# w_down in two column blocks at a time, with seven products for eight in half of its pairs of k-tiles

## The chip, the core and the metric

The kernel runs on one core of a Trainium2 chip. The metric is the time of one execution on the device, in microseconds (us). Five engines work side by side: TensorE (PE, matrix products), VectorE (DVE), ScalarE (ACT), GpSimd (POOL) and SyncE (SP). Each takes its own instructions in the order in which the program issues them, and waits on semaphores for the others. SP issues nearly all loads of weights, POOL issues the transfers that add to what they find.

## The reference

One block of a streaming encoder, for x of 256 rows (S) by 2048 columns (D), in float32. First `h = x + W_out [attention ; convolution](rms_norm(x))`, and then the part that changes, the gated feed-forward network with 5632 hidden columns:

```python
hn   = rms_norm(h, norm2_g)
gate = hn @ w_gate            # 256 x 5632, k = 2048
up   = hn @ w_up              # 256 x 5632, k = 2048
a    = silu(gate) * up
out  = h + a @ w_down         # 256 x 2048, k = 5632
```

## The kernel before

**Three matmuls for a product.** Every float32 operand is split into a high part in the matmul's own type (a cast on ACT) and a low part (DVE subtracts the cast from the original). A product of a k-tile (128 rows of k) is three matmuls of 128 x 128 by 128 x 512: high by high, low by high, high by low.

**Columns and groups.** w_gate and w_up are taken in 11 blocks `j` of 512 columns, w_down in four blocks `n` of 512. The hidden columns are used in groups of 4, 4 and 3 blocks (`FGROUPS`): gate and up of j = 0 to 3, then w_down over their 16 k-tiles for all four `n`; then j = 4 to 7 and w_down; then j = 8 to 10 and w_down over 12 k-tiles. The result gathers in DRAM: it holds h first, and the first two groups add their share by an accumulating DMA on POOL's queue (`down_done`, L1034, after a copy on ACT, L1033). The last group instead fetches what is there (`fetch_sums`, L1025, on SP's queue, ahead of the loads that follow it), adds on DVE (L1043) and writes.

**Seven products for eight.** In the blocks j = 1 to 10 four pairs of k-tiles are computed by a scheme that needs seven block products for the eight of a 2 x 2 block product (rows: the two halves of 128 rows; columns: gate and up). Such an "s" unit loads four weight tiles at once (`load_pair`, L898, tile `wb`, 1 MB). DVE forms four sums of them (`round_pair`, L907 to L909, tile `wt`), ACT casts the three tiles of `wb` that are used directly and the four sums (L910, L911, tile `wh`), DVE takes the seven low parts (`split_pair`, L915 for those of `wb`, L916 for the sums, tile `wl`), and PE runs 21 matmuls (L932 to L934) into seven PSUM banks. The left side of these products is prepared once, by `make_forms` (tiles `fhi`, `flo`). The rest of a block are plain units of two k-tiles and 12 matmuls, "g" for gate and "u" for up. A capital letter in `ORDER = "sgGsgGsUUsUu"` marks a unit whose low part is made by DMA: ACT writes the negated original, and POOL's queue adds the original to the cast from DRAM. A block is 180 matmuls. At its end DVE combines the banks (`products_done`, L995 to L1004, and `block_done`, L1013, L1015).

**Transposes.** The block's result `a` must stand with k on the partitions for w_down. `transposed` does that two k-tiles at a time during the next block: PE transposes four tiles into one bank (`ps_a`, L827), ACT casts the high part (`ahi`, L829), DVE takes the low part (`alo`, L831).

**w_down** uses plain units alone: 12 matmuls for two k-tiles (L356, L357, L362), one block of columns after another, all low parts on DVE (L326).

**The order of the work.** All units stand in one list, and `run_chunks` goes through it. At step t it issues the load of unit t + 5, for a capital unit also the cast and the accumulating DMA of unit t + 5, the cast of unit t + 3, the low parts of unit t + 2, and the matmuls of unit t. The ends of blocks and the transposes are generators, which move one step each time PE's code calls `resume()`, several times in a unit. So the order on each engine is set when the program is written, and an operation that waits holds up all that stands behind it on its engine.

**Buffers.** Two `wb`, one `wt`, two `wh`, two `wl`, five `raw` (loads of plain units), four each of `whi` and `wlo`. All eight PSUM banks are in use: four `acc`, four `aux`, of which the transposes take one while a block is under way.

Of the kernel before, what the change touches and what calls it, by code (L numbers as in the profile page):

```python
# [18 lines left out]
P = 128  # L19
# [38 lines left out]
RAW_BUFS = 5  # L58
# [24 lines left out]
PRODUCTS = ((Q1, 0, 5), (Q6, 5, 1), (Q7, 6, 2), (Q5, 4, 3), (Q2, 1, 6), (Q4, 3, 0), (Q3, 2, 4))  # L83

LOAD_AHEAD, DMA_AHEAD, HI_AHEAD, LO_AHEAD = 5, 5, 3, 2
# [15 lines left out]
def tile_block(  # L101
# [11 lines left out]
    lhs = ctx.enter_context(tc.tile_pool(name="lhs", bufs=KD // 2))  # L113
# [95 lines left out]

    halves = {}  # L210
# [6 lines left out]
    def lhs_two(pfx, k):  # L217
        return tuple(lhs.tile([P, 2, S], F32R, tag=f"l{x}", name=f"{pfx}{x}{k}") for x in ("hi", "lo"))
# [165 lines left out]
    def run_chunks():  # L384
        n = len(chunks)
        loaded = split = 0
# [14 lines left out]
        for t in range(n):  # L401
# [17 lines left out]
            if t in fetch_at:  # L419
                fetch_sums(fetch_at[t])  # L420
# [336 lines left out]
    def out_done(n, ps):  # L757
# [28 lines left out]
        if n == D // N - 1:  # L786
            yield
            for m in range(NM):
                ss = small.tile([P, 1], F32, tag="ssh", name="ssh")
                dve.tensor_reduce(ss, ss2[m], AX.X, ALU.add)  # L790
                rsqrt_mean(rstd2[m], ss, D, EPS)
            yield
            yield
            prestack.close()
            ffn["pool"] = ctx.enter_context(tc.tile_pool(name="ffn", bufs=1))
            start(make_forms())
# [22 lines left out]

    def transposed(j, aa):  # L820
        for t in range(N // P // 2):
# [6 lines left out]
            hi, lo = lhs_two("a", j * (N // P) + 2 * t)  # L828
            act.copy(hi, pt)  # L829
            yield from lag(2)  # L830
            dve.tensor_tensor(lo, pt, hi.bitcast(F32), ALU.subtract)  # L831
            for i in range(2):
                actT[j * (N // P) + 2 * t + i] = (hi[:, i, :], lo[:, i, :])
            yield from lag(2 if j else 1)

    forms = {}

    def make_forms():  # L840
# [33 lines left out]
        f = fp.tile([P, 7, NS, P], F32, tag="wh", name="sums", bufs=2)  # L874
        dve.scalar_tensor_tensor(f[:, 4], a21, -1.0, a22, ALU.mult, ALU.subtract)
        dve.scalar_tensor_tensor(f[:, 5], f[:, 4], -1.0, a11, ALU.mult, ALU.subtract)
        act.copy(fhi[:, 0], a11)
        act.copy(fhi[:, 1], a12)
        act.activation(fhi[:, 3], a22, AF.Copy, scale=-1.0)
        yield  # L880
        dve.tensor_tensor(f[:, 6], a11, a21, ALU.subtract)
        dve.tensor_tensor(f[:, 2], a12, f[:, 5], ALU.subtract)
        act.copy(fhi[:, 4:7], f[:, 4:7])
        act.copy(fhi[:, 2], f[:, 2])
# [4 lines left out]
        dve.scalar_tensor_tensor(flo[:, 3], a22, -1.0, fhi[:, 3].bitcast(F32), ALU.mult, ALU.subtract)  # L889
        dve.tensor_tensor(flo[:, 2], f[:, 2], fhi[:, 2].bitcast(F32), ALU.subtract)  # L890
        yield
        dve.tensor_tensor(flo[:, 4:7], f[:, 4:7], fhi[:, 4:7].bitcast(F32), ALU.subtract)
        forms.update(hi=fhi, lo=flo)

    def load_pair(c):
        c["b"] = early.tile([P, 4, N], F32, tag="wb", name="wb")
        src = weights([(w, k, c["col"], N) for w in ("w_up", "w_gate") for k in (c["k"], c["k"] + HK)])
# [14 lines left out]

    def split_pair(c):
        c["lo"] = ffn["pool"].tile([P, 7, N], F32R, tag="wl", name="wl", bufs=2)
        dve.tensor_tensor(c["lo"][:, 4:], c["b"][:, 1:], c["hi"][:, 4:].bitcast(F32), ALU.subtract)  # L915
        dve.tensor_tensor(c["lo"][:, :4], c["t"], c["hi"][:, :4].bitcast(F32), ALU.subtract)  # L916
# [8 lines left out]
    def multiply_pair(c):  # L925
        while "hi" not in forms:
            resume()
        fhi, flo, p = forms["hi"], forms["lo"], c["k"]
        for n, (q, f, w) in enumerate(c["products"]):
# [4 lines left out]
            pe.matmul(ps, fhi[:, f, p, :], c["lo"][:, w], start=False, stop=bool(last))  # L934
# [6 lines left out]
    def multiply_two(c):  # L941
        hi, lo = c["hi"], c["lo"]
        qs = (Q3, QX) if c["kind"] == "u" else (Q2, Q4)
        for i, k in enumerate(c["ks"]):
            x1, x2 = forms["plain"][k]
            for m, q in enumerate(qs):
                ms = slice(m * P, (m + 1) * P)
                ps = sum_bank(c, q)
                pe.matmul(ps, x1[:, ms], hi[:, i, :], start=i == 0 and bool(c["first"].get(q)), stop=False)  # L949
                pe.matmul(ps, x2[:, ms], hi[:, i, :], start=False, stop=False)  # L950
        resume()
        for m, q in enumerate(qs):
            ms = slice(m * P, (m + 1) * P)
            for i, k in enumerate(c["ks"]):
                pe.matmul(sum_bank(c, q), forms["plain"][k][0][:, ms], lo[:, i, :], start=False,  # L955
                          stop=i == 1 and bool(c["last"].get(q)))
# [4 lines left out]
    def fast_block(j, order, after_down):  # L961

        units, sums = [], {}
        left = dict(s=list(range(NS)), g=list(TWOS), u=list(TWOS))
        for unit in order:
            kind = unit.lower()
            what = left[kind].pop(0)
            c = dict(kind=kind, sums=sums, done=None, first={}, last={})
            if kind == "s":
                c.update(k=what, col=j * N, by_dma=False, load=load_pair, round=round_pair, split=split_pair,  # L970
                         multiply=multiply_pair, uses=[q for q, _, _ in PRODUCTS], products=PRODUCTS)
            else:
                c.update(ks=what, w="w_gate" if kind == "g" else "w_up", nk=2, width=N, cols=[(j * N, N)],
                         by_dma=unit.isupper(),
                         load=load_chunk, round=round_chunk, split=split_chunk, multiply=multiply_two,
                         uses=(Q3, QX) if kind == "u" else (Q2, Q4))
            units.append(c)
        assert not any(left.values())
        if after_down:

            units[0]["products"] = PRODUCTS[4:] + PRODUCTS[:4]
        for q in range(8):
            users = [c for c in units if q in c["uses"]]
            users[0]["first"][q] = users[-1]["last"][q] = True
        [c for c in units if c["kind"] == "s"][-1]["done"] = products_done
        units[-1].update(done=lambda sums: block_done(j, sums), prompt=True)
        chunks.extend(units)
# [3 lines left out]
    def products_done(q):  # L991
# [11 lines left out]
        act.activation(w1, w1, AF.Silu)  # L1003
        dve.tensor_tensor(u3, q[Q4], u3, ALU.add)  # L1004
        act.activation(u3, u3, AF.Silu)
        halfway.update(g=(w1, u3), u=(u2, w4))

# [11 lines left out]
    so_far, fetch_at = {}, {}  # L1019

    def fetch_sums(n):
        so_far[n] = []
        for m in range(NM):
            t = ffn["pool"].tile([P, N], F32, tag=f"sum{n % 2 * NM + m}", name="so_far")
            sp.dma_start(out=t, in_=out[m * P : (m + 1) * P, n * N : (n + 1) * N])  # L1025
            so_far[n].append(t)

    def down_done(g, n, ps):
        cs = slice(n * N, (n + 1) * N)
        if g < len(FGROUPS) - 1:  # L1030
            for m in range(NM):
                t = ffn["pool"].tile([P, N], F32, tag=f"sum{n % 2 * NM + m}", name="part")
                act.copy(t, ps[m])  # L1033
                pool.dma_start(out=out[m * P : (m + 1) * P, cs], in_=t, accum_op=ALU.add)  # L1034
            return
        parts = 2 if n == D // N - 1 else 1
        for m in range(NM):
            t = so_far[n][m]
# [89 lines left out]
```

## Time and profile before

| | |
|---|---|
| time, median of 3 runs | 1079.25 us (1078.09 to 1081.81) |
| profiled execution | 1078.51 us, of which the profile's span is 1076.7 us |
| PE busy | 1051.7 us, 98% of the span |
| DVE busy | 801.4 us, 74% |
| ACT busy | 618.0 us, 57% |
| POOL busy | 110.4 us, 10% |
| TensorE clock granted | 0.995 of full speed |
| data moved by DMA | 236.57 MB, 220 GB/s in the mean |

Times are in microseconds from the span's start unless marked otherwise. L912 is line 912 of the kernel before, or, in rows of the changed kernel, of that one; the two are numbered apart. In a row such as `out<-in`, the names are the program's tiles; `q` are the PSUM banks of a gate/up block, `acc` those of a w_down unit. A busy PE need not be a PE at its peak, since matmuls overlap; the step from one start to the next is what a matmul costs.

### The profile page before, as it was taken

To read this page: it belongs to the slowest core of one execution; us is meant where nothing else is said; L and a number is where in the kernel's file an instruction comes from. 1 tells how busy PE (TensorE), PEld (TensorE's weight loads), DVE (VectorE), ACT (ScalarE), POOL (GpSimd) and SP (SyncE) were. 2 spreads that over 40 slices of the span, in tenths; PEclk is the share of its full clock that TensorE was granted. 3 is DMA by queue.
4 is the path that set the end of the run, shared out by engine and by line. 5 is a ranking of instruction groups with operands and counts; after the bars stand their busy time and mean duration, and the time that the engine had idled before them with its cause. 6 is when DMAs were issued, how large, how long until landed. Compare 5 with 4: busy or idle time off the path is not lost. (4 is left out here: it accounts for less than half of the span.)

```text
span 1076.7 us, 13151 instructions
## 1 busy us (share of the span) xinstructions
PE 1051.7 (98%) x4834; PEld 870.9 (81%) x4834; DVE 801.4 (74%) x979; ACT 618.0 (57%) x811; POOL 110.4 (10%) x155
## 2 busy tenths in 40 slices
PE   8999999999999999999999999999999999999798
PEld 7988888877888887788888878878888878888686
DVE  4799988899666689988644688889745477897353
ACT  6544566756756557757343667586544474765231
POOL 0130112200100100101000111010001010100000
PEclk9999999999999999999999999999999999999899
DMA  9555555344457568898476898988847799887471
GB/s 314 205 176 180 200 189 176 137 176 151 143 190 242 175 228 252 284 304 244 153 232 197 267 295 252 293 221 268 259 157 201 239 277 319 223 273 208 145 278 66
DMA packets 62781, 236.57 MB, mean 220 GB/s; under 512 B 7044, under 2 KB 8510, under 8 KB 57596
## 3 DMA queue, kind: packets, MB, share of 16 engines
q1 hardware_dynamic: 52320, 202.66, 52.1%
q0 software_dynamic: 10336, 33.04, 16.6%
q8 instruction: 38, 0.62, 0.2%
q14 instruction: 27, 0.22, 0.1%
q10 hardware_dynamic: 60, 0.03, 0.0%
HBM read 227.30 MB, written 8.39 MB: 219 GB/s over the span
## 5 line engine op out<-in xcount | busy, mean ns | idle before, releaser
L317 ACT CAST whi<-raw 128x1024 fp32r<-128x1024 f32 (+1 forms) x297 | 305.8, 1050 | 183.2 <-PE acc L357 98.1
L326 DVE TENSOR_TENSOR wlo<-raw,whi 128x1024 fp32r<-128x1024 f32 (+1 forms) x249 | 299.7, 1219 | 142.8 <-ACT whi L317 140.9
L357 PE MATMUL acc<-whi,alo 128*128 128x512 f32 x384 | 150.5, 392 | 6.6 <-DVE alo L831 6.6
L356 PE MATMUL acc<-whi,ahi 128*128 128x512 f32 x384 | 150.4, 392 | 0.0
L356 PE MATMUL acc<-whi,xhi 128*128 128x512 f32 (+1 forms) x352 | 131.0, 378 | 3.2 <-ACT xhi L223 2.4
L357 PE MATMUL acc<-whi,xlo 128*128 128x512 f32 (+1 forms) x352 | 129.5, 374 | 0.5 <-DVE xlo L224 0.4
L949 PE MATMUL q<-whi,chi 128*128 128x512 f32 x320 | 124.7, 390 | 0.0
L950 PE MATMUL q<-whi,clo 128*128 128x512 f32 x320 | 124.6, 389 | 0.0
L932 PE MATMUL q<-wh,fhi 128*128 128x512 f32 x280 | 109.7, 392 | 1.7 <-DVE alo L831 1.7
L934 PE MATMUL q<-wl,fhi 128*128 128x512 f32 x280 | 109.0, 389 | 0.0
L933 PE MATMUL q<-wh,flo 128*128 128x512 f32 x280 | 109.0, 389 | 0.0
L512 DVE SCALAR_TENSOR_TENSOR y<-upad,cw,y 128x256 f32<-128x256 f32 x240 | 103.7, 483 | 4.4 <-ACT y L505 3.9
L362 PE MATMUL acc<-wlo,ahi 128*128 128x512 f32 x384 | 103.6, 391 | 0.0
L911 ACT CAST wh<-wt 128x2048 fp32r<-128x2048 f32 x40 | 76.5, 1912 | 38.3 <-DVE wt L909 37.6
L916 DVE TENSOR_TENSOR wl<-wt,wh 128x2048 fp32r<-128x2048 f32 x40 | 91.7, 2291 | 6.6 <-ACT wh L911 5.9
L915 DVE TENSOR_TENSOR wl<-wb,wh 128x1536 fp32r<-128x1536 f32 x40 | 70.1, 1754 | 27.9 <-ACT wh L910 27.9
L357 PEld LDWEIGHTS acc<-whi,alo 128*128 128x128 f32 x384 | 72.6, 189 | 22.1 <-DVE alo L831 6.9
L362 PE MATMUL acc<-wlo,xhi 128*128 128x512 f32 (+1 forms) x352 | 88.3, 376 | 1.4 <-DVE wlo L326 1.4
L955 PE MATMUL q<-wlo,chi 128*128 128x512 f32 x320 | 86.6, 392 | 2.8 <-DMA wlo<-in_wts_dram 2.8
L356 PEld LDWEIGHTS acc<-whi,ahi 128*128 128x128 f32 x384 | 72.5, 189 | 15.3 <-ACT ahi L829 0.2
L362 PEld LDWEIGHTS acc<-wlo,ahi 128*128 128x128 f32 x384 | 71.7, 188 | 14.6
L356 PEld LDWEIGHTS acc<-whi,xhi 128*128 128x128 f32 x352 | 67.2, 191 | 14.9 <-ACT xhi L223 2.8
(197 smaller groups left out, 1487.2 us busy)
## 6 DMA issues: line engine op xcount, KB each, us to landing
raw<-in_wts_dram SPq DMA_DIRECT2D x295, 512.0 KB, 4.9
wb<-in_wts_dram SPq DMA_DIRECT2D x40, 1024.0 KB, 6.2
wlo<-in_wts_dram POOLq DMA_DIRECT2D x48, 512.0 KB, 8.3
out_dram<-part POOLq DMA_DIRECT2D x16, 256.0 KB, 5.1
out_dram<-h POOLq DMA_DIRECT2D x8, 256.0 KB, 5.9
so_far<-out_dram SPq DMA_DIRECT2D x8, 256.0 KB, 4.4
h<-in_x_dram SPq DMA_DIRECT2D x6, 256.0 KB, 7.6
out_dram<-so_far POOLq DMA_DIRECT2D x6, 256.0 KB, 3.0
```

Source lines behind the costliest of these rows:

```text
L317: act.copy(c["hi"], c["raw"])
L326: dve.tensor_tensor(c["lo"], c["raw"], c["hi"].bitcast(F32), ALU.subtract)
L356: pe.matmul(ps[m], xhi[:, ms], hi[:, j, :], start=c["first"] and j == 0, stop=False)
L357: pe.matmul(ps[m], xlo[:, ms], hi[:, j, :], start=False, stop=False)
L362: pe.matmul(ps[m], xhi[:, ms], lo[:, j, :], start=False, stop=c["last"] and j == nk - 1)
L512: dve.scalar_tensor_tensor(y[:, ct, :], src, wk, y[:, ct, :], ALU.mult, ALU.add)
L916: dve.tensor_tensor(c["lo"][:, :4], c["t"], c["hi"][:, :4].bitcast(F32), ALU.subtract)
L932: pe.matmul(ps, fhi[:, f, p, :], c["hi"][:, w], start=bool(first), stop=False)
L933: pe.matmul(ps, flo[:, f, p, :], c["hi"][:, w], start=False, stop=False)
L934: pe.matmul(ps, fhi[:, f, p, :], c["lo"][:, w], start=False, stop=bool(last))
L949: pe.matmul(ps, x1[:, ms], hi[:, i, :], start=i == 0 and bool(c["first"].get(q)), stop=False)
L950: pe.matmul(ps, x2[:, ms], hi[:, i, :], start=False, stop=False)
```

## The change

1. w_down takes two blocks of columns at a time (`down_block`). The two take the place of up and gate in a block: four pairs of k-tiles in each of the first two groups and three in the last become s units with seven products for eight, the other half stays plain. The matmuls of w_down go from 1056 to 990, and there are 62 s units in all instead of 40. Some of the plain units have their low parts by DMA now (capitals in `DOWN`): 72 in the whole program instead of 48.
2. The transposed result that goes into an s unit of w_down needs forms like those of `make_forms`. `pair_forms` makes them: ACT copies the bank out (`af`), casts three of its quarters, DVE forms four sums (`fs`), ACT casts these, DVE takes the low parts.
3. The low parts of an s unit are split in two tiles that are made at two times. `split_pair` makes four of them (`wla`, two buffers: one of `wb`, three of the sums), `split_rest` the other three (`wlb`, one buffer: one of the sums, two of `wb`). `split_rest` is called one unit ahead of the unit's matmuls, or by the next `round_pair` if that comes first.
4. All groups add their sums to DRAM by POOL's accumulating DMA, but for the last block of columns of the last group: its sum so far is fetched by one DMA of 512 KB on POOL's queue (`down_products`), added on DVE and written by SP. Copies on ACT before the accumulating DMAs are gone.
5. The order of the products after a w_down group is no longer turned round; two of the seven left forms change places; there are four `raw` buffers instead of five; the left side's tiles stand in one fixed array.

```diff
-RAW_BUFS = 5
+RAW_BUFS = 4
-PRODUCTS = ((Q1, 0, 5), (Q6, 5, 1), (Q7, 6, 2), (Q5, 4, 3), (Q2, 1, 6), (Q4, 3, 0), (Q3, 2, 4))
+PRODUCTS = ((Q1, 0, 5), (Q6, 5, 1), (Q7, 6, 2), (Q5, 4, 3), (Q2, 1, 6), (Q4, 2, 0), (Q3, 3, 4))
+DOWN = (dict(pairs=((0, 0), (0, 1), (1, 0), (1, 1)), order="sgGsgGsUusUu"),
+        dict(pairs=((4, 0), (4, 1), (5, 0), (5, 1)), order="sgGsgGsUusUu"),
+        dict(pairs=((8, 0), (8, 1), (9, 0)), order="sgGsGsUuU"))
...
@@ run_chunks
-            if t in fetch_at:
-                fetch_sums(fetch_at[t])
+            while rest < min(n, t + 1 + REST_AHEAD):
+                split_rest(chunks[rest])
+                rest += 1
             chunks[t]["multiply"](chunks[t])
...
@@ transposed
+            if (j, t) in d["pairs"]:
+                yield from pair_forms(j, t, pt)
+            else:
+                hi, lo = d["at"][j, t]
+                act.copy(hi, pt)
+                yield from lag(2)
+                dve.tensor_tensor(lo, pt, hi.bitcast(F32), ALU.subtract)
...
+    def pair_forms(j, t, pt):
...
+        a = fp.tile([P, 2, NM, P], F32, tag="sum0", name="af")
+        act.copy(a, pt)
+        a11, a21, a12, a22 = a[:, 0, 0], a[:, 0, 1], a[:, 1, 0], a[:, 1, 1]
+        act.copy(fhi[:, :2], a[:, :, 0])
+        act.activation(fhi[:, 2], a22, AF.Copy, scale=-1.0)
+        yield
+        f = fp.tile([P, 4, P], F32, tag="sum2" if j else "sum1", name="fs")
+        dve.scalar_tensor_tensor(f[:, 1], a21, -1.0, a22, ALU.mult, ALU.subtract)
+        dve.scalar_tensor_tensor(f[:, 2], f[:, 1], -1.0, a11, ALU.mult, ALU.subtract)
+        dve.tensor_tensor(f[:, 3], a11, a21, ALU.subtract)
+        dve.tensor_tensor(f[:, 0], a12, f[:, 2], ALU.subtract)
+        act.copy(fhi[:, 3:], f)
+        yield
+        dve.tensor_tensor(flo[:, :2], a[:, :, 0], fhi[:, :2].bitcast(F32), ALU.subtract)
+        dve.scalar_tensor_tensor(flo[:, 2], a22, -1.0, fhi[:, 2].bitcast(F32), ALU.mult, ALU.subtract)
+        yield
+        dve.tensor_tensor(flo[:, 3:], f, fhi[:, 3:].bitcast(F32), ALU.subtract)
...
     def round_pair(c):
+        if newest:
+            split_rest(newest.pop())
+        newest.append(c)
...
     def split_pair(c):
-        c["lo"] = ffn["pool"].tile([P, 7, N], F32R, tag="wl", name="wl", bufs=2)
-        dve.tensor_tensor(c["lo"][:, 4:], c["b"][:, 1:], c["hi"][:, 4:].bitcast(F32), ALU.subtract)
-        dve.tensor_tensor(c["lo"][:, :4], c["t"], c["hi"][:, :4].bitcast(F32), ALU.subtract)
+        if "lo" in c:
+            return
+        b, t, hi = c["b"], c["t"], c["hi"].bitcast(F32)
+        lo = ffn["pool"].tile([P, 4, N], F32R, tag="wla", name="wla", bufs=2)
+        dve.tensor_tensor(lo[:, 0], b[:, 2], hi[:, 5], ALU.subtract)
+        dve.tensor_tensor(lo[:, 1:], t[:, 1:], hi[:, 1:4], ALU.subtract)
...
+    def split_rest(c):
+        if "sides" not in c or 0 in c.get("lo", ()):
+            return
+        split_pair(c)
+        b, t, hi = c["b"], c["t"], c["hi"].bitcast(F32)
+        lo = ffn["pool"].tile([P, 3, N], F32R, tag="wlb", name="wlb")
+        dve.tensor_tensor(lo[:, 1], t[:, 0], hi[:, 0], ALU.subtract)
+        dve.tensor_tensor(lo[:, ::2], b[:, 1::2], hi[:, 4::2], ALU.subtract)
...
+    def down_block(g, n):
...
+        units = fast_block(DOWN[g]["order"], ("w_down", n * N), ("w_down", (n + 1) * N),
+                           [(q, ks(jt)) for q, jt in enumerate(pairs)], [(jt, ks(jt)) for jt in twos],
...
-    def fetch_sums(n):
-        so_far[n] = []
-        for m in range(NM):
-            t = ffn["pool"].tile([P, N], F32, tag=f"sum{n % 2 * NM + m}", name="so_far")
-            sp.dma_start(out=t, in_=out[m * P : (m + 1) * P, n * N : (n + 1) * N])
...
+    def down_products(n, q, last):
+        so_far = None
+        if last:
+            so_far = ffn["pool"].tile([P, 4, N], F32, tag="wt", name="so_far")[:, :NM]
+            pool.dma_start(out=so_far, in_=out[:, n * N : (n + 1) * N].rearrange("(m p) n -> p m n", p=P))
+        yield from bank_sums(q)
+        for m in range(NM):
+            add_to_out(m, n + 1, halfway["g"][m])
...
     for g, nb in enumerate(FGROUPS):
...
-        for n in range(D // N):
-            block("w_down", n * N, range(j0 * 4, (j0 + nb) * 4), fa, lambda ps, g=g, n=n: down_done(g, n, ps))
+        for n in range(0, D // N, 2):
+            down_block(g, n)
```

Three places show how the rows move. The first is DVE in the gate/up block j = 4, from its first s unit on. Before:

```order
L907 TENSOR_TENSOR wt<-wb 128x1024
L908 TENSOR_TENSOR wt<-wb,wt 128x512
L909 TENSOR_TENSOR wt<-wt,wb 128x512
L915 TENSOR_TENSOR wl<-wb,wh 128x1536
L916 TENSOR_TENSOR wl<-wt,wh 128x2048
L326 TENSOR_TENSOR wlo<-raw,whi 128x1024
```

And in the changed program:

```order
L964 TENSOR_TENSOR wt<-wb 128x1024
L965 TENSOR_TENSOR wt<-wb,wt 128x512
L966 TENSOR_TENSOR wt<-wt,wb 128x512
L978 TENSOR_TENSOR wla<-wb,wh 128x512
L979 TENSOR_TENSOR wla<-wt,wh 128x1536
L337 TENSOR_TENSOR wlo<-raw,whi 128x1024
L988 TENSOR_TENSOR wlb<-wt,wh 128x512
L989 TENSOR_TENSOR wlb<-wb,wh 128x2x512
```

Between the last sum and the first low part that needs the cast sums there stood 1536 columns of other work (L915), now there stand 512 (L978); two of the three pieces on `wb` come last (L989).

The second place is DVE at the start of the last w_down group, from the end of the last gate/up block on. Before (`alo` are the low parts of that block's transposes):

```order
L1015 TENSOR_TENSOR sum_8332<-sum_8332,sum_8331 128x512
L1015 TENSOR_TENSOR sum_8334<-sum_8334,sum_8333 128x512
L326 TENSOR_TENSOR wlo<-raw,whi 128x1024 x4
L831 TENSOR_TENSOR alo_8420<-ps_a,ahi_8419 128x512
L326 TENSOR_TENSOR wlo<-raw,whi 128x1024 x2
L831 TENSOR_TENSOR alo_8469<-ps_a,ahi_8468 128x512
```

And in the changed program, where `llo` is what `alo` was:

```order
L1127 TENSOR_TENSOR sum_8559<-sum_8559,sum_8558 128x512
L1127 TENSOR_TENSOR sum_8561<-sum_8561,sum_8560 128x512
L964 TENSOR_TENSOR wt<-wb 128x1024
L965 TENSOR_TENSOR wt<-wb,wt 128x512
L966 TENSOR_TENSOR wt<-wt,wb 128x512
L978 TENSOR_TENSOR wla<-wb,wh 128x512
L979 TENSOR_TENSOR wla<-wt,wh 128x1536
L988 TENSOR_TENSOR wlb<-wt,wh 128x512
L989 TENSOR_TENSOR wlb<-wb,wh 128x2x512
L964 TENSOR_TENSOR wt<-wb 128x1024
L965 TENSOR_TENSOR wt<-wb,wt 128x512
L966 TENSOR_TENSOR wt<-wt,wb 128x512
L867 TENSOR_TENSOR llo<-ps_a,lhi 128x512
```

The first transposed tiles' low part (L867) stands behind one s unit's sums and low parts and the sums of the next.

The third place is ACT in the block j = 5, around the second group of its transposes. Before:

```order
L910 CAST wh<-wb 128x1536
L911 CAST wh<-wt 128x2048
L829 CAST ahi_5943<-ps_a 128x512
L317 CAST whi<-raw 128x1024
L320 ACTIVATE wlo<-raw 128x1024
```

And in the changed program, with `pair_forms`:

```order
L967 CAST wh<-wb 128x1536
L968 CAST wh<-wt 128x2048
L877 COPY af<-ps_a 128x512
L879 CAST lhi<-af 128x2x128
L880 ACTIVATE lhi<-af 128x128
L887 CAST lhi<-fs 128x4x128
L328 CAST whi<-raw 128x1024
```

One cast out of the bank has become a copy and three casts, of which the last needs DVE's sums (L887 behind `fs`), and all stand behind the cast of the unit's weight sums (L968).

More of the change, by code (lines that the diff above doesn't have):

```diff
@@ L925, in multiply_pair @@
     def multiply_pair(c):
-        while "hi" not in forms:
+        while not c["ready"](c):
             resume()
-        fhi, flo, p = forms["hi"], forms["lo"], c["k"]
-        for n, (q, f, w) in enumerate(c["products"]):
+        (fhi, flo), p = c["forms"](), c["p"]
+        for n, (q, f, w) in enumerate(PRODUCTS):
             ps = sum_bank(c, q)
@@ new lines, in down_done @@
+    def down_done(n, q, last):
+        while "added" not in halfway:
+            yield
+        halfway.pop("added")
+        halfway.pop("g")
+        u = halfway.pop("u")
+        parts = 2 if last else 1
+        w = N // parts
+        for m, i in enumerate((Q3, QX)):
+            for part in range(parts):
+                ws = slice(part * w, (part + 1) * w)
+                dve.tensor_tensor(u[m][:, ws], q[i][:, ws], u[m][:, ws], ALU.add)
+                if last:
+                    sp.dma_start(out=out[m * P : (m + 1) * P, n * N + part * w : n * N + (part + 1) * w], in_=u[m][:, ws])
+            if last and m == 0:
+                yield
+        if not last:
+            for m in range(NM):
+                add_to_out(m, n, u[m])
```

187 lines of the change are left out of this document (109 added, 78 removed).

## The prediction

> **What bounds the kernel now.** I read the page first, for the share of each engine.
>
> ```profile
> span 1076.7 us, 13151 instructions
> PE 1051.7 (98%) x4834; PEld 870.9 (81%) x4834; DVE 801.4 (74%) x979; ACT 618.0 (57%) x811; POOL 110.4 (10%) x155
> ```
>
> PE is busy for 98%. The profiled execution took 1078.51 us, 1.8 more than its span and 0.74 less than the median of the runs. The view of waits (released engine, releaser, total us, times, longest) then says when PE stood still in the part that changes:
>
> ```profile
> PE acc L357 <- DVE alo L831: 6.6, 1, 6.6
> PE q L955 <- DMA wlo<-in_wts_dram: 2.8, 2, 1.7
> ```
>
> That is little: one stall in the last w_down group, and a few us on loads. Two consecutive starts of the first matmul of a gate/up block (timeline) give a block, and two starts inside a paired unit's 21 matmuls give one matmul:
>
> ```profile
> 656.81 0.39 PE L932 MATMUL q<-wh,fhi 128*128 128x512 f32 x1
> 698.73 0.39 PE L932 MATMUL q<-wh,fhi 128*128 128x512 f32 x1
> ...
> 441.58 0.39 PE L932 MATMUL q<-wh,fhi 128*128 128x512 f32 x1
> 446.34 0.39 PE L949 MATMUL q<-whi,chi 128*128 128x512 f32 x1
> ```
>
> A block takes 41.92 us; 21 matmuls take 4.76, so one takes 0.2267, and the block's 180 take 40.8. The other 1.1 are its two groups of transposes. PE sets the pace today. How near is the next engine? The windows view, for a stretch of gate/up and w_down together:
>
> ```profile
> core 0: us, PE busy (x) PEld busy (x) DVE busy (x) ACT busy (x) POOL busy (x), PEclk, DMA share, GB/s
> 614.00:780.00 166.00, 163.62 (x732) 134.66 (x731) 137.33 (x129) 109.72 (x102) 19.11 (x22) 1.00 0.89 264
> ```
>
> DVE is busy for 83%, but the share hides its waits, so I followed DVE through one paired unit (timeline; in brackets the wait and its releaser):
>
> ```profile
> 417.42 1.23 DVE L907 TENSOR_TENSOR wt<-wb 128x1024 f32<-128x1024 f32 x1
> 418.68 0.69 DVE L908 TENSOR_TENSOR wt<-wb,wt 128x512 f32<-128x512 f32 x1
> 419.40 0.69 DVE L909 TENSOR_TENSOR wt<-wt,wb 128x512 f32<-128x512 f32 x1
> 420.01 1.75 DVE L915 TENSOR_TENSOR wl<-wb,wh 128x1536 fp32r<-128x1536 f32 x1
> 420.13 1.92 ACT L911 CAST wh<-wt 128x2048 fp32r<-128x2048 f32 x1 [2.00 <-DVE wt L909]
> 422.08 2.29 DVE L916 TENSOR_TENSOR wl<-wt,wh 128x2048 fp32r<-128x2048 f32 x1 [0.32 <-ACT wh L911]
> 424.41 1.22 DVE L907 TENSOR_TENSOR wt<-wb 128x1024 f32<-128x1024 f32 x1
> ```
>
> The weight sums take 2.59 (417.42 to 420.01). ACT can only then cast them, and DVE can take their low parts at 422.08, 2.07 later. Today the 1.67 of L915 fill that gap, and the unit's period is 6.99.
>
> **The change, part by part.**
>
> *Products removed.* 22 w_down units of 24 matmuls become 22 of 21: 66 fewer. 66 x 0.2267 = **15.0 us** less PE work. This is the gain if PE stays the bound.
>
> *The low parts in another order.* Their elements are the same, but in the changed program's DVE order L978 (512 wide), which alone stands between the sums L966 and L979, is all that fills the gap; the other two pieces on wb (L989) come behind. L978 takes 0.60 (the step between the 0.68 us operations below), so DVE idles 1.47. A unit is then 2.59 + 2.07 + 1.67 (L979, as wide as L915) + 0.60 + 1.13 (L988, L989 by widths) = **8.06**, 1.07 longer. There are 62 such units instead of 40.
>
> What else DVE does in a block, from the end of one:
>
> ```profile
> 479.79 0.68 DVE L997 TENSOR_TENSOR sum<-q,sum 128x512 f32<-128x512 f32 x1
> 481.19 1.22 DVE L326 TENSOR_TENSOR wlo<-raw,whi 128x1024 fp32r<-128x1024 f32 x1
> 482.32 0.68 DVE L1000 TENSOR_TENSOR sum<-q,sum 128x512 f32<-128x512 f32 x1
> ...
> 484.72 1.28 DVE L1013 TENSOR_TENSOR sum<-q,sum 128x512 f32<-128x512 f32 x2
> 485.91 1.28 DVE L1015 TENSOR_TENSOR sum<-sum,sum 128x512 f32<-128x512 f32 x2
> 487.11 1.22 DVE L907 TENSOR_TENSOR wt<-wb 128x1024 f32<-128x1024 f32 x1
> ```
>
> A low part of a plain unit is 1.13; sums and block end together are 487.11 - 479.79 - 1.13 = 6.2. A gate/up block without transposes needs 4 x 8.06 + 3 x 1.13 + 6.2 = **41.8** of DVE, against PE's 40.8. A w_down pair of columns has the same sums without the 1.2 of L1015 and four low parts: 41.76. So each block is already past PE.
>
> *Transposes.* The plain kind stays; its second subtract stands between sums and low parts:
>
> ```profile
> 673.94 0.69 DVE L831 TENSOR_TENSOR alo<-ps_a,ahi 128x512 fp32r<-128x512 f32 x1 [2.45 <-ACT ahi L829]
> L829 ACT CAST ahi<-ps_a 128x512 fp32r<-128x512 f32 x22 | 12.8, 581 | 24.7 <-PE ps_a L827 24.7
> L692 DVE SCALAR_TENSOR_TENSOR wt<-pr,r,p 128x128 f32<-128x128 f32 x4 | 1.4, 347 | 0.0
> ```
>
> The first costs 0.60. The second waits 2.45, in which the cast of the sums ends too: 2.45 + 0.60 + 0.60 + 1.67 + 1.73 + 2.59 = 9.64 for that unit, 1.6 more than 8.06. A block with plain transposes needs **44.1**. The pair forms (new) have no row. Their four 128-wide sums cost between 4 x 0.27 (347 ns less the 0.08 by which 0.68 us operations follow at 0.60) and 4 x 0.60, the 512-wide step; I take 1.1, being of that width; the low parts add 1.2 by widths. In the first transposes that is 2.2. In the second, ACT's order has the copy L877 behind the cast L968: 2.07 + 0.58 until DVE may form the sums, then 1.1 + 0.6 + 0.60 + 1.67 + 0.6 + 1.73, with 2.59 ahead 11.4, 3.3 more than 8.06. Such a block needs **47.3**; by the upper price 50.
>
> *From j=2 to the last gate/up block.* These are 13 blocks: pair forms in j=2, 5, 6, 9 (4 x 47.3), plain transposes in j=3, 7 (2 x 44.1), none in j=4, 8 (2 x 41.8), one of each in j=10 (45.6), four w_down pairs of columns, two with transposes (2 x 44.0 + 2 x 41.76): **578.1**.
>
> ```profile
> 445.79 1.22 DVE L907 TENSOR_TENSOR wt<-wb 128x1024 f32<-128x1024 f32 x1
> 475.77 1.76 DVE L915 TENSOR_TENSOR wl<-wb,wh 128x1536 fp32r<-128x1536 f32 x1 [0.99 <-ACT wh L910]
> ...
> 996.74 1.07 PE L955 MATMUL q<-wlo,chi 128*128 128x512 f32 x4
> 998.60 1.28 DVE L1015 TENSOR_TENSOR sum<-sum,sum 128x512 f32<-128x512 f32 x2
> ```
>
> DVE enters j=2 at 445.79 today; j=1 gains 4 x 1.07 and pair forms of about 5: 454.8. The last block then ends on DVE at 1032.9, against 999.9 (998.60 + 1.28). Tried on the block from 445.79 to 487.11, this adding gives 4 x 6.99 + 3 x 1.13 + 6.2 + 0.6 + 2.7 = 40.9, and the block, 41.32 less the 0.68 net that DVE waited at 475.77 for a buffer of PE's, needed 40.6: 0.25 too much, 3.3 over 13 blocks.
>
> *The end.* Today's stall, with the rows of its chain:
>
> ```profile
> 999.41 12.27 SPq L1025 DMA_DIRECT2D so_far<-out_dram  x2
> 1011.73 0.90 SPq L313 DMA_DIRECT2D raw<-in_wts_dram  x2
> 1016.28 1.04 ACT L317 CAST whi<-raw 128x1024 fp32r<-128x1024 f32 x1 [4.23 <-DMA raw<-in_wts_dram]
> 1018.50 0.68 DVE L831 TENSOR_TENSOR alo<-ps_a,ahi 128x512 fp32r<-128x512 f32 x1
> ```
> ```profile
> 1012.20 0.40 PE L356 MATMUL acc<-whi,ahi 128*128 128x512 f32 x1
> ...
> 1019.24 0.80 PE L357 MATMUL acc<-whi,alo 128*128 128x512 f32 x1 [6.64 <-DVE alo L831]
> ...
> 1023.29 0.39 PE L356 MATMUL acc<-whi,ahi 128*128 128x512 f32 x1
> ...
> 1071.81 0.61 PE L362 MATMUL acc<-wlo,ahi 128*128 128x512 f32 x2
> ```
>
> The fetch sat 12.27 us in SP's queue, loads behind it came late, and the unit took 11.09 instead of 12 x 0.2267 = 2.72: **8.4** lost, 1.5 of it because the 11 matmuls from 1019.24 ran slowly. Moving the fetch to POOL's queue removes that cause. But in the new DVE order L867, which the third unit's second matmul needs, stands behind the sums, both low parts and the next sums. From the last block's DVE end X: 2.59 + 2.07 + 1.67 + 1.73 + 2.59 + 0.69 = X + 11.3, while PE gets there at X + 5.3 (its last gate/up matmul is done at 996.74 + 4 x 0.2267 = 997.6, 2.2 before that end, and 33 matmuls, 7.5, come first): a stall of 6 and 1.5 of slow matmuls. Then 2.5 for that unit, 0.5 transposes, 20.4 (90 matmuls), 30.6 (135), 1.5, and 4.3 from the last matmuls to the span's end (1076.7 - 1072.4): X + 71.1 = 1104.0, less 3.3: 1100.7. **Sum: 1100.7 + 1.8 = 1102 us.**
>
> *At nothing.* Of the raw buffers only four are taken between two wb loads anyway. The 24 added accumulates on POOL's queue are issued five units ahead, some 17 us, and need 8.3 (row below); without that cover PE would wait for them, up to 1.7 each by the wait on L955 above, 40 in all. The 512 KB fetch has three units (8.2 us) behind it.
>
> ```profile
> wlo<-in_wts_dram POOLq DMA_DIRECT2D x48, 512.0 KB, 8.3
> wb<-in_wts_dram SPq DMA_DIRECT2D x40, 1024.0 KB, 6.2
> ```
>
> **The rivals.**
>
> *B: PE stays the bound* (faster). DVE's busy time per block rises by one or two us only, and 83% leaves room for it. If other DVE work falls into the gaps, or ACT casts sooner, so that a unit costs at most 7.4 (PE's 13 blocks are 540.3, DVE's 574.8: 2.65 a block, 0.66 a unit), then 1078.5 - 15.0 - 0.9 (8.4 at the end becomes 7.5) = 1063. Against it: nothing else stands between L978 and L979 in the order. The Trainium skill, page "Perfetto Trace Analysis", section "Identifying the Most-Contended Engine", ranks engines by occupancy and takes a vector engine's occupancy as a fair measure of its nearness to its limit; by that rule PE stays ahead and B holds, and the rows above differ from it, since DVE's gap is no occupancy.
>
> *C: only the pair-form blocks exceed PE.* With a unit at 7.4, those blocks still need 44.7 against 41.9: four times 2.8, 1.1 in j=10, about 5 in j=1: +17.3. 1078.5 - 15.9 + 17.3 = 1080.
>
> *D: loads bind.* A wb buffer is now read until L989, and is loaded again only then: 6.2 + casts and sums + 8.06, about 16 of the 22 us in which two units follow. It decides from a landing of 12 us, twice the row; then some 1115.
>
> **How the numbers follow.** Forecast 0.60 (its own range 1085 to 1113: 0.25 us less a unit takes off 13, the upper price of the forms adds 12), B 0.25, C 0.12, D 0.03. The measurement tells 0.3% (3.2 us) from no change. Faster: B and a quarter of C, 0.28; within: half of C and the forecast's lowest edge, 0.08; slower: 0.64. Range 1058 to 1112: it reaches to B and its spread, leaving about 0.05 below and 0.1 above.
>
> **What would show it.** Right: DVE waits for ACT at L979 some 1.4 us in nearly each of 62 units; blocks of 42 to 47 us instead of 41.9, the longest in j=5, 6, 9; PE waits in the paired units for wla and wlb, and in the last group for L867. Wrong: blocks of 41 to 42 with PE unbroken (B), or DVE waiting on wb loads (D).

## The result, and the profile after

The changed kernel takes 1156.84 us (median, 1155.07 to 1158.86) against 1079.28 before: a ratio of 1.0716, 95% interval 1.0689 to 1.0743. It is slower, as forecast, but by 77.6 us and not by 23, and outside the range. The profiled execution has a span of 1156.0 us. The page:

```profile
span 1156.0 us, 13323 instructions
PE 1080.6 (93%) x4768; PEld 869.8 (75%) x4768; DVE 912.5 (79%) x1252; ACT 674.0 (58%) x857; POOL 132.9 (11%) x180
```

The 66 matmuls are gone, and PE stands still for 75 us instead of 25. It is busy 28.9 us longer all the same; the granted clock is 0.973 in the mean instead of 0.995. Where the time went is read from the ends of the gate/up blocks on DVE (timeline; first, three about the first w_down group, last):

```profile
463.63 1.28 DVE L1127 TENSOR_TENSOR sum<-sum,sum 128x512 f32<-128x512 f32 x2
...
557.92 1.28 DVE L1127 TENSOR_TENSOR sum<-sum,sum 128x512 f32<-128x512 f32 x2
697.90 1.28 DVE L1127 TENSOR_TENSOR sum<-sum,sum 128x512 f32<-128x512 f32 x2
747.98 1.28 DVE L1127 TENSOR_TENSOR sum<-sum,sum 128x512 f32<-128x512 f32 x2
...
1081.03 1.28 DVE L1127 TENSOR_TENSOR sum<-sum,sum 128x512 f32<-128x512 f32 x2
```

| piece of the span | forecast | measured | difference |
|---|---|---|---|
| up to DVE's end of j = 1 | 454.8 | 464.9 | +10.1 |
| the 13 blocks to the last gate/up block | 574.8 | 617.4 | +42.6 |
| from there to the end | 71.1 | 73.7 | +2.6 |

The three differences make the 55.3 us by which 1156.0 exceeds the 1100.7 of the sum. Most of it lies in the blocks: the three from 557.92 to 697.90, two pairs of w_down columns and j = 4, were to take 44.0, 41.8 and 41.8, and take 46.7 each. DVE's waits in those 617 us say what stood in between (waits view of that stretch):

```profile
DVE wla L979 <- ACT wh L968: 56.0, 43, 1.4
DVE wla L978 <- ACT wh L967: 26.2, 11, 5.7
DVE wlo L337 <- ACT whi L328: 11.8, 4, 5.3
...
DVE wt L964 <- DMA wb<-in_wts_dram: 3.4, 2, 2.2
```

The first row is the gap that was forecast; so were the waits of the transposes, which are not shown (22.1 us in nine). The other three, 41.4 us, were not. A wait of the second kind isn't new in itself. In the kernel before, DVE waited for the cast of wb too, between the ends of j = 1 and j = 10 (446 to 1000 us; the second row is ACT in the same stretch):

```profile
DVE wl L915 <- ACT wh L910: 27.8, 12, 4.7
ACT whi L317 <- DMA raw<-in_wts_dram: 30.3, 8, 5.5
```

There PE was busy for 549 of 554 us, so the time that DVE waited was to spare; now DVE sets the pace. The length of a wait thus doesn't give its price, which the experiments have to show. What has grown is ACT's wait for the raw loads. ACT and SP in the changed kernel's stretch:

```profile
ACT whi L328 <- DMA raw<-in_wts_dram: 100.9, 24, 9.8
...
SPq L952 <- DVE wlb L989: 545.8, 53, 15.1
```

SP spends 546 of 617 us at a wb load that waits until L989 has read the buffer, with the plain loads behind it. One turn of this loop, in the block j = 4 (timeline rows of DVE, SP, ACT and PE put in order of time):

```profile
658.97 1.22 DVE L989 TENSOR_TENSOR wlb<-wb,wh 128x1024 fp32r<-128x1024 f32 x1
660.25 0.33 SPq L952 DMA_DIRECT2D wb<-in_wts_dram  x1
...
667.03 1.22 DVE L989 TENSOR_TENSOR wlb<-wb,wh 128x1024 fp32r<-128x1024 f32 x1
668.32 0.33 SPq L952 DMA_DIRECT2D wb<-in_wts_dram  x1
668.70 0.90 SPq L324 DMA_DIRECT2D raw<-in_wts_dram  x2
670.45 1.23 DVE L964 TENSOR_TENSOR wt<-wb 128x1024 f32<-128x1024 f32 x1 [2.20 <-DMA wb<-in_wts_dram]
673.98 1.05 ACT L328 CAST whi<-raw 128x1024 fp32r<-128x1024 f32 x1 [9.26 <-DMA raw<-in_wts_dram]
675.90 1.46 ACT L967 CAST wh<-wb 128x1536 fp32r<-128x1536 f32 x1
677.39 0.69 DVE L978 TENSOR_TENSOR wla<-wb,wh 128x512 fp32r<-128x512 f32 x1 [4.27 <-ACT wh L967]
679.19 1.76 DVE L979 TENSOR_TENSOR wla<-wt,wh 128x1536 fp32r<-128x1536 f32 x1 [1.11 <-ACT wh L968]
681.00 0.79 PE L1008 MATMUL q<-wla,fhi 128*128 128x512 f32 x1 [1.06 <-DVE wla L979]
```

L989 is the last reader of wb. SP issues the next wb load only then (660.25, 668.32), and two raw loads behind it. DVE waits for the first of these wb loads until 670.45. ACT needs a raw load of 668.70 for a unit whose low part is made by DMA, and that cast stands ahead of the cast of the s unit's weights. So DVE, which could go on, waits 4.27 us, and PE after it. Loads wait for DVE and DVE for loads.

### The profile page after: what moved, and what is told of

The parts are those of the page before. It is cut to its first block, busy times and chain, and to the rows that moved or that the text cites. A ratio compares the mean times of both kernels' runs of the same rounds, so it can differ in the third digit from the quotient of the medians.

```text
span 1156.0 us, 13323 instructions
## 1 busy us (share of the span) xinstructions
PE 1080.6 (93%) x4768; PEld 869.8 (75%) x4768; DVE 912.5 (79%) x1252; ACT 674.0 (58%) x857; POOL 132.9 (11%) x180
## 5 line engine op out<-in xcount | busy, mean ns | idle before, releaser
L328 ACT CAST whi<-raw 128x1024 fp32r<-128x1024 f32 (+1 forms) x253 | 260.2, 1045 | 167.8 <-DMA raw<-in_wts_dram 125.6
L337 DVE TENSOR_TENSOR wlo<-raw,whi 128x1024 fp32r<-128x1024 f32 (+1 forms) x181 | 219.0, 1217 | 57.0 <-ACT whi L328 56.6
L968 ACT CAST wh<-wt 128x2048 fp32r<-128x2048 f32 x62 | 118.3, 1908 | 101.9 <-DVE wt L966 101.9
L367 PE MATMUL acc<-whi,lhi 128*128 128x512 f32 (+1 forms) x448 | 170.8, 386 | 3.3 <-ACT lhi L234 2.6
L368 PE MATMUL acc<-whi,llo 128*128 128x512 f32 (+1 forms) x448 | 169.1, 382 | 0.5 <-DVE llo L235 0.4
L979 DVE TENSOR_TENSOR wla<-wt,wh 128x1536 fp32r<-128x1536 f32 x62 | 108.9, 1757 | 64.3 <-ACT wh L968 64.3
L1025 PE MATMUL q<-whi,clo 128*128 128x512 f32 x320 | 124.6, 389 | 0.0
L373 PE MATMUL acc<-wlo,lhi 128*128 128x512 f32 (+1 forms) x448 | 116.4, 384 | 0.0
L367 PEld LDWEIGHTS acc<-whi,lhi 128*128 128x128 f32 x448 | 85.3, 190 | 20.7 <-ACT lhi L234 2.8
L368 PEld LDWEIGHTS acc<-whi,llo 128*128 128x128 f32 x448 | 85.4, 191 | 17.7 <-DVE llo L235 0.9
L373 PEld LDWEIGHTS acc<-wlo,lhi 128*128 128x128 f32 x448 | 79.9, 189 | 16.9 <-DVE wlo L337 0.2
L967 ACT CAST wh<-wb 128x1536 fp32r<-128x1536 f32 x62 | 90.8, 1465 | 2.9 <-PE q L1007 1.5
L331 ACT ACTIVATE wlo<-raw 128x1024 fp32r<-128x1024 f32 x72 | 76.0, 1055 | 0.0
L989 DVE TENSOR_TENSOR wlb<-wb,wh 128x1024 fp32r<-128x1024 f32 x62 | 75.5, 1218 | 0.0
```

The costliest lines, as they stand in the source:

```text
L328: act.copy(c["hi"], c["raw"])
L337: dve.tensor_tensor(c["lo"], c["raw"], c["hi"].bitcast(F32), ALU.subtract)
L367: pe.matmul(ps[m], xhi[:, ms], hi[:, j, :], start=c["first"] and j == 0, stop=False)
L368: pe.matmul(ps[m], xlo[:, ms], hi[:, j, :], start=False, stop=False)
L373: pe.matmul(ps[m], xhi[:, ms], lo[:, j, :], start=False, stop=c["last"] and j == nk - 1)
L968: act.copy(c["hi"][:, :4], t)
```

## The experiments

Two theories were set against each other. **A**: the split of the low parts is the cause, by the gap at L979 and by the late release of wb. **B** (in these texts, not the prediction's B): the w_down side is, that is pair forms, more s units, more DVE work. Ratios are to the kernel before.

**One part alone: the split in the kernel before.** `split_pair` and `split_rest` are those of the change; nothing on w_down.

```diff
-        c["lo"] = ffn["pool"].tile([P, 7, N], F32R, tag="wl", name="wl", bufs=2)
...
+        lo = ffn["pool"].tile([P, 4, N], F32R, tag="wla", name="wla", bufs=2)
...
+            while rest < min(n, t + 1 + REST_AHEAD):
+                split_rest(chunks[rest])
+                rest += 1
```

> The kernel before with one part of the change: the low parts of an s unit in two tiles and at two times as in the changed kernel (wla with one piece of wb and three of the sums, wlb one unit later). w_down, its sums and its fetch are as before. Theory A: the 40 gate/up units have the gap (1.4 us each) and the late wb loads: gate/up blocks of 44 to 47 us instead of 41.9, 1100 to 1125 us. Rival B: 1079 to 1085 us.

1119.59 us, 1.0355 (1.0334 to 1.0375): 39 us for the split alone, with the old w_down.

```profile
DVE wla L928 <- ACT wh L917: 36.5, 29, 1.4
DVE wla L927 <- ACT wh L916: 32.9, 13, 3.5
```

These are the two waits again, here on L928 and L927, between 445 and 1045 us (the block j = 5 takes 45.6, j = 6 46.4). The first was 5.0 us in the kernel before (L916). The second is only 5 us above the 27.8 there, so this run shows the cost of the split, but not how much of it is the loads'. It is what A expected and rules B out as the main cause.

**The loads alone.** In `run_chunks` the two plain loads that follow a wb load go ahead of it:

```diff
+        load_order = list(range(n))
+        for i in range(n - 2):
+            if (an s unit and two plain ones at i, i + 1, i + 2):
+                load_order[i : i + 3] = [i + 1, i + 2, i]
         def load(i):
+            i = load_order[i]
```

> The changed kernel with the two plain loads that follow a wb load put ahead of it in SP's queue; nothing on DVE, ACT or PE moves. SP waits 546 us at wb loads for L989, and the plain loads behind them come late. Load loop as the cause of the part that the DVE sum left out (41 us): ACT's waits for raw (101 us in the stretch) mostly go, DVE's waits at L978 and L337 with them, the stretch falls from 617 to about 577, time 1110 to 1125 us; the gap at L979 stays at 1.37 us. If the loads are only late because DVE is late: no change, 1150 to 1160 us.

1122.05 us, 1.0387 (1.0371 to 1.0402): 34.8 less than the changed kernel, with the same instructions in the same order on DVE, ACT and PE. Waits from 450 to 1055 us:

```profile
DVE wla L985 <- ACT wh L974: 61.9, 45, 1.4
...
DVE wt L970 <- DMA wb<-in_wts_dram: 7.4, 6, 3.0
...
ACT whi L328 <- DMA raw<-in_wts_dram: 4.1, 3, 2.4
```

ACT's wait for raw fell from 101 to 4 us, the waits at the wb cast are gone, the gap (L985 here) stays. The load loop is shown as a cause by itself. And now the blocks are what DVE's chain alone makes them:

```profile
461.75 1.28 DVE L1133 TENSOR_TENSOR sum<-sum,sum 128x512 f32<-128x512 f32 x2
508.82 1.28 DVE L1133 TENSOR_TENSOR sum<-sum,sum 128x512 f32<-128x512 f32 x2
553.35 1.29 DVE L1133 TENSOR_TENSOR sum<-sum,sum 128x512 f32<-128x512 f32 x2
```

47.07 for j = 2 with pair forms and 44.53 for j = 3 with plain transposes; the prediction had 47.3 and 44.1 less 0.25. From DVE's end of j = 1 to that of j = 10 the run takes 585.3 us, against 617.4 in the changed kernel and 574.8 in the sum. Of the 10.5 that stay, 8.6 lie in the two stretches from a group's last gate/up block over w_down to the next block's end (131.0 and 131.3 where 126.8 had been worked out), in which DVE still waits 6.7 us for wb.

**The gap alone.** ACT casts each piece of the sums as soon as it stands:

```diff
-        act.copy(c["hi"][:, :4], t)
+        act.copy(c["hi"][:, 2:4], t[:, 2:])
+        act.copy(c["hi"][:, 1], t[:, 1])
+        act.copy(c["hi"][:, 0], t[:, 0])
```

> The changed kernel with ACT's cast of the sums in three pieces, each as soon as its sum stands; DVE's order is as in the changed kernel. The gap before L979 falls from 1.37 to about 0.1 us in each of 62 units, and wb is let go only as much earlier. Theory A with the gap alone as its cause: 65 to 80 us less, 1077 to 1092 us. With the load loop as the larger part: the waits at L978 and L337 stay near 40 us, 1095 to 1130 us. Rival B: as the changed kernel less the idle time that the gap itself is, 1100 or more, with pair-form blocks longest.

1123.32 us, 1.0397 (1.0378 to 1.0416): 33.5 less. Waits from 450 to 1055 us:

```profile
DVE wla L980 <- ACT wh L967: 38.1, 11, 5.1
DVE wlo L337 <- ACT whi L328: 22.0, 4, 8.3
DVE wla L981 <- ACT wh L969: 10.6, 14, 0.8
...
ACT whi L328 <- DMA raw<-in_wts_dram: 139.9, 28, 11.0
```

The gap shrinks to 10.6 us, and a part of what it gave is taken back by the loads, for which ACT waits longer than in the changed kernel. The time alone fits two of the three expectations, the load loop as the larger part and B; the run before this one and the next decide between them.

**Both mends.** The last two diffs together, in the changed kernel.

> The changed kernel with both edits: the cast of the sums in three pieces and the two plain loads ahead of the wb load. Theory A (gap at L979 and late loads are the two causes, and little else): with the loads swapped alone the stretch from the first to the last fast block was 585 us, all of it DVE's chain; 52 gaps of 1.3 less make 518 of DVE, below PE's 540, so PE is the bound but in the pair-form blocks: 1065 to 1080 us. Rival: casts in three delay ACT or the pair forms stay the bound: 1085 to 1110 us.

1077.69 us, 0.9972 (0.9951 to 0.9992): 79 us less than the changed kernel, more than the two alone add up to (68). PE is the bound again:

```profile
450.00:1010.00 560.00, 554.20 (x2453) 452.45 (x2451) 505.54 (x621) 385.59 (x461) 68.74 (x79) 1.00 0.91 266
```

(columns as in the window rows of the prediction: PE busy 554 of 560 us.) w_down keeps its seven products, its pair forms and its accumulates in this run. The slowdown lies in the split and its order, not in the idea. Both mends in the kernel before without the split were not run; but PE stands still there for 25 us in all, so they could not give 79.

**The old order of the low parts, in the new tiles.** `split_pair` takes the two pieces of wb of `wlb` first and the piece of the sums last, wherever the matmuls of the s unit before are already issued; `split_rest` does what is left.

```diff
+        rest = ffn["pool"].tile([P, 3, N], F32R, tag="wlb", name="wlb")
+        dve.tensor_tensor(rest[:, ::2], b[:, 1::2], hi[:, 4::2], ALU.subtract)
         dve.tensor_tensor(lo[:, 0], b[:, 2], hi[:, 5], ALU.subtract)
         dve.tensor_tensor(lo[:, 1:], t[:, 1:], hi[:, 1:4], ALU.subtract)
+        dve.tensor_tensor(rest[:, 1], t[:, 0], hi[:, 0], ALU.subtract)
```

> The changed kernel with the low parts of an s unit in the order that the kernel before has: the two pieces on wb that stood last (L989) stand first, the piece of the sums right behind L979, all in one step. Theory A (the split of the low parts holds it up: DVE's idle gap at L979, 56 us of the 617 from the first to the last fast block, and wb read to the end of the chain, so that the next wb load and the loads behind it come late, 41 us of DVE waits at L978, L337 and L964): both go, a unit's DVE chain is 6.9 instead of 8.0 us, blocks fall from 47 to 41 to 43 us, time 1065 to 1090 us. Rival B (the w_down side is at fault: pair forms, more s units, DVE work as such): the blocks with pair forms stay at 47 and over, and the time at 1110 or more.

1128.88 us, 1.0449 (1.0433 to 1.0465): 28 us less only, a miss. The time and the blocks with pair forms (47.5 to 48.2) are even those that B expected. But a new wait took the place of the old ones:

```profile
DVE wlb L980 <- PE q L1019: 38.2, 21, 3.5
```

There is one `wlb` buffer, so DVE now waits for PE's last product of the unit before, and may not work ahead. It isn't a clean undo, and so no test of B; a second `wlb` buffer was not tried.

**The mended split in the kernel before.** The diff of the split in the kernel before and those of both mends; the loads are swapped only where the five units before are fast ones.

> The kernel before with the split of the low parts (1119.6 us) and both mends, cast in three and loads swapped where the units before are fast ones too. Theory A: the 39 us that the split cost go, 1078 to 1088 us. If the split costs by something else (one wlb buffer, the later step of the last pieces), 1095 or more.

1092.08 us, 1.0098 (1.0076 to 1.0121): 27.5 of the 39 us come back; the time lies between the two expectations, 4 us over A's. Gate/up blocks behind one another are at 41.8 again (711.45 to 753.22 for the ends of j = 5 and j = 6 on DVE); what is left is 8 us in j = 1 and 2.8 in each stretch from a group's last gate/up block over w_down to the next group's first (134.8 against 132.0). What causes it there stays open.

**The fetch alone, in the kernel before.**

```diff
-            sp.dma_start(out=t, in_=out[m * P : (m + 1) * P, n * N : (n + 1) * N])
+            pool.dma_start(out=t, in_=out[m * P : (m + 1) * P, n * N : (n + 1) * N])
```

> The kernel before with one part of the change: the sums so far are fetched on POOL's queue instead of SP's; nothing else moves. Theory: the 6.6 us stall on the transposes' low part in the last group and the slow matmuls behind it (8.4 together) go: 1070 to 1074 us. Rival: something else on DVE or ACT is late next and the stall stays: 1077 to 1081 us.

1075.29 us, 0.9942 (0.9919 to 0.9966).

```profile
1017.17 0.50 PE L357 MATMUL acc<-whi,alo 128*128 128x512 f32 x1 [2.31 <-DVE alo L831]
```

The stall falls from 6.64 to 2.31 us, and the time by 6 instead of 8.4, which lies between the two expectations. The fetch in the load queue caused the larger part of the stall; a wait for DVE remains.

**What is left in the mended kernel.** Three steps on top of one another, on the run with both mends: the first group's pairs from j = 1 and 2; then the last block's transposes two steps earlier, and their low part right behind ACT's cast; then that for j = 0 too.

```diff
-DOWN = (dict(pairs=((0, 0), (0, 1), (1, 0), (1, 1)), order="sgGsgGsUusUu"),
+DOWN = (dict(pairs=((1, 0), (1, 1), (2, 0), (2, 1)), order="sgGsgGsUusUu"),
```
```diff
-        yield from lag(TO_TRANSPOSE)
+        yield from lag(3 if j == sum(FGROUPS) - 1 else TO_TRANSPOSE)
...
-                yield from lag(2)
+                yield from lag(0 if j == sum(FGROUPS) - 1 else 2)
```
```diff
-                yield from lag(0 if j == sum(FGROUPS) - 1 else 2)
+                yield from lag(0 if j in (0, sum(FGROUPS) - 1) else 2)
```

> The kernel with both mends (1077.7 us), and the pairs of the first group are taken from j = 1 and 2 instead of 0 and 1, so that the block j = 1 has plain transposes and no pair forms. With both mends that block ends on DVE at 457.4 us, the kernel before at 445.8: PE waits 4.9 there for the copy out of the transposes' bank and runs slowly after. If the pair forms in j = 1 are the reason: 5 to 10 us less, 1068 to 1073 us. If it is the two s units at a distance of two and the single wlb buffer: no change, 1076 to 1079 us.

> The run with pairs from j = 1 on, and besides the last block's transposes two steps earlier and their low part right behind ACT's cast, so that it stands on DVE behind the first sums instead of behind two units' sums and low parts. In the run with both mends PE waits 2.2 and 3.7 us there and runs slowly after, about 7.5 in all. If that order on DVE is the cause of the stall at the end: 5 to 7 us less than the run with the pairs from j = 1. If something else is late next (ACT's cast, the wla low parts): 0 to 3 us less.

> The run with the earlier transposes at the end (1071.3 us), and the low parts of the first block's transposes (j = 0) too right behind ACT's cast. In the run before PE waits 4.1 us at 420 us for that low part, which stands on DVE behind the sums of the second s unit, and runs slowly for some 11 matmuls after: 6.5 in all. If the place of that low part is what makes j = 1 long: 3 to 6 us less, 1065 to 1068 us (wla of the second unit is late next, 1 to 2 us). If the s units at a distance of two are: 0 to 1 us less.

1077.65, 1071.28 and 1067.92 us. The first changed nothing: in j = 1 PE waits 3.8 us for the plain low part where it waited 4.9 for the copy, so the pair forms weren't the reason. The second gave 6.4: the order on DVE was the end's stall. The third gave 3.4: a part of what j = 1 costs. The last of them takes less time than both kernels, 0.9878 of the kernel before (0.9851 to 0.9905).

**Two small parts, in the kernel before.** The left side's tiles in one fixed array; and one raw buffer less.

```diff
-        return tuple(lhs.tile([P, 2, S], F32R, tag=f"l{x}", name=f"{pfx}{x}{k}") for x in ("hi", "lo"))
+        at = slot[0] % (KD // 2) * 4
+        slot[0] += 1
+        return tuple(a[:, at : at + 4].rearrange("p (k m) c -> p k (m c)", k=2) for a in arena)
```
```diff
-RAW_BUFS = 5
+RAW_BUFS = 4
```

> The kernel before with one small part of the change: the left side's tiles stand in one fixed array for the high and one for the low parts, instead of eight tiles of a pool each. In the changed kernel and in all runs made from it the first matmul of j = 1 starts at 401 to 403 us, before at 397.8, and the matmuls of the projections ahead of it step at 0.234 to 0.239 us instead of 0.228 to 0.235. If the array is the cause: j = 1 at about 402, 1083 to 1086 us. If not: 397.8 and 1079 to 1081 us.

> The kernel before with four raw buffers instead of five, nothing else. If the fifth buffer was what kept the part ahead of j = 1 at its pace: j = 1 starts at about 402 us, 1083 to 1086 us. As predicted for this part (nothing): 397.8 and 1079 to 1081 us.

1092.30 us, 1.0111 (1.0074 to 1.0147), and 1086.41 us, 1.0056 (1.0031 to 1.0081). The prediction put the buffer at nothing and has no term for the array. The array first (start of j = 1 on PE in the kernel before and in this one; then PE from 100 to 200 us in both):

```profile
397.81 0.39 PE L949 MATMUL q<-whi,chi 128*128 128x512 f32 x1
100.00:200.00 100.00, 100.00 (x465) 83.02 (x463) 92.32 (x166) 60.89 (x137) 17.69 (x22) 1.00 0.49 174
```
```profile
401.95 0.40 PE L953 MATMUL q<-whi,chi 128*128 128x512 f32 x1
100.00:200.00 100.00, 100.00 (x448) 81.08 (x447) 91.67 (x166) 59.64 (x136) 15.07 (x22) 1.00 0.50 174
```

PE is busy for all of the 100 us at the full granted clock in both, and does 448 matmuls instead of 465. No engine's wait shows; the mean step between two 512-wide matmuls that follow without a wait is 0.234 us instead of 0.227 (timeline, 354 steps in each). The rest of its 11 us comes with the w_down groups: the first two stretches over w_down grow from 132.0 to 135.0 and 134.7, the last group to the end by 2.9. With four raw buffers j = 1 starts at 398.40, 0.6 later; 3 us are lost in j = 1, 2.1 and 1.0 in the two stretches over w_down, and PE's waits for low parts by DMA are up from 2.8 to 5.3 us.

## Why the prediction was wrong

- **The gap at L979: right.** 1.3 us in each of 43 of the stretch's 52 units (56.0 / 43; 1.47 forecast); in the other nine the transposes wait instead, as the sum had it. With the loads out of the way a pair-form block takes 47.07 us where 47.05 had been worked out, j = 10 takes 45.6 where 45.35 had been.
- **The end: right in its place, 1.7 us too small.** L1025 starts 11.3 us after the last block's DVE end, the number of the sum. The stall is 7.7 instead of 6, in two pieces, of which the first, for ACT's `lhi`, was not in the sum:

```profile
1089.27 0.79 PE L1024 MATMUL q<-whi,lhi 128*128 128x512 f32 x1 [4.17 <-ACT lhi L865]
1093.61 0.80 PE L1025 MATMUL q<-whi,llo 128*128 128x512 f32 x1 [3.55 <-DVE llo L867]
```

- **The step that failed is rival D's**, "about 16 of the 22 us in which two units follow. It decides from a landing of 12 us". That wb is let go late was right; the period was wrong, and so was the path. 22 us is a mean over a block. At a block's start DVE takes s units back to back, 9.2 us apart (650.91, 660.10). So from the end of L989 of one unit (660.19) to the sums of the next but one (DVE is ready for them at 668.25) there were about 8 us, not 22 less 16 plus a landing of 6, and the load landed 10.2 after its issue. Even so DVE waits only 3.4 us for wb itself. D did not count that the raw loads queue behind wb, and that ACT's casts for the DMA units, issued five units ahead, stand ahead of the cast that DVE waits for; by that path come the other 38.0 of the 41.4 us. The blocks were missed by 42.6; in them the swap of the loads gives 32.1 back, and 34.8 in the whole time.
- **D stood as an alternative to the forecast**, with 0.03. But a later release of wb follows from the same order that makes the gap. The two add up; they don't exclude each other, and both together are the 79 us that the two mends return.
- **"At nothing" failed for the raw buffers**, which cost 5 us when taken alone, and **the fixed array had no term at all**: alone in the kernel before it costs 11 us, and PE begins j = 1 4.1 later with it (401.95), where the changed kernel begins it too (401.88). That is 4.1 of the 10.1 us that j = 1 was late. How much these two cost in the changed kernel, where DVE and loads hide part of it, was not measured.
- **Products removed, and rival B's 1063.** With gap and loads mended PE is the bound and the time is 1077.7. The 15 us of products are there, but lost elsewhere. From DVE's end of the group's last gate/up block to that of the next group's first the run takes 125.9 and 124.6 us, the kernel before 132.0 each (24 matmuls fewer, 5.4 by the sum); all 13 blocks take 545.6 instead of 554.0, and the end 71.8 instead of 76.8. Against that DVE ends j = 1 at 457.8 instead of 445.9. Taken alone in the kernel before, the array and the raw buffer make 3.9 and 3.6 there. Moving the last block's and the first block's transposes forward brought the time to 1067.9.
- **Rival C** (only the pair forms) is out: j = 3 and j = 7, which have no pair forms, rose from 41.1 and 41.0 us to 46.5 and 45.7.
- **Two small sums** of the prediction are off: the terms of a pair-form unit's chain add up to 11.5 and not 11.4, and a block with plain transposes to 44.0 and not 44.1. Together that is 0.6 us of the stretch and changes nothing.

## What to carry to other kernels

When an operation moves to the end of a unit, price what it still holds: here the last reader of a load's buffer, and with it every load in that queue. Compare the time from that release to the next use in the densest stretch of the schedule, not in the mean. Order queues so that a load that must wait for its buffer stands behind those that need not.

## What was not expected of the hardware

A left operand in another place made matmuls some 3% longer (mean step 0.227 to 0.234 us between 100 and 200 us, 0.227 to 0.231 between 300 and 395) at an unchanged granted clock; what in the array's place or form does it stays open.

After some waits of 2 to 3 us PE runs at half pace for a while, after others not. In the changed kernel, after 2.14 us of waiting:

```profile
1026.80 0.39 PE L1008 MATMUL q<-wla,fhi 128*128 128x512 f32 x1
1029.33 0.80 PE L1006 MATMUL q<-wh,fhi 128*128 128x512 f32 x1 [2.14 <-DVE sum L1110]
1029.92 0.63 PE L1007 MATMUL q<-wh,flo 128*128 128x512 f32 x1
1030.35 0.63 PE L1008 MATMUL q<-wla,fhi 128*128 128x512 f32 x1
...
1032.76 0.39 PE L1008 MATMUL q<-wlb,fhi 128*128 128x512 f32 x1
```

The steps are 0.43 us instead of 0.23 until 1032.5, and the granted clock from 1029.3 to 1032.5 is 0.50, where it was 1.00 from 1024 to 1027. But waits of 2.59 us (at 648.65) and 3.11 us (at 794.97 and 1078.78) were followed by steps of 0.23 and a granted clock of 1.00. So the length of the wait alone does not decide; what does stays open. The Trainium skill, page "TensorE: Matmul & The Clock Gate", section "HAM oscillation — how this bites in real kernels", puts the rule as no idle gaps of PE above some 3.4 us; here 2.14 us were enough once, so by this row the rule is not tight.
